# Narrow TensorE tiles for the small products of a delta-rule decoder layer

## The chip, the cores and the metric

The kernel runs on one core of a Trainium2 chip. The metric is the time of one execution on the device, in microseconds (us). The median of three runs before the change is 1135.75 us (1135.46 to 1139.98). TensorE (PE in the rows; PEld is its weight load) multiplies, VectorE (DVE), ScalarE (ACT) and GpSimd (POOL) work on elements, SyncE (SP) issues most loads.

## What is computed

One layer of a decoder for a prompt of 512 tokens with 16 learned meta tokens in front, and for 8 samples of 8 new tokens each. The layer has differential attention and a gated delta rule side by side on one normalised input, gates that merge them, and a gated feed-forward net with a short convolution. The change lies in the delta rule. It has 4 heads, and per head a matrix state of 128 by 128 for the prompt and one for each of the 8 samples. Cut to what matters:

```python
def l2norm(x):
    return xf * lax.rsqrt(jnp.sum(xf * xf, axis=-1, keepdims=True) + 1e-6)

qkv, new_gdn_conv = causal_dwconv(gdn_qkv, gdn_conv_buf, p['gdn_conv_w'])   # its last 3 rows are an output
qkv = jax.nn.silu(qkv)
gq = l2norm(gq) * (GDN_DK ** -0.5)
gk = l2norm(gk)
beta = jax.nn.sigmoid(gdn_b)
g = -jnp.exp(a_log) * jax.nn.softplus(gdn_a + dt_bias)
...
gcum = jnp.cumsum(gc, axis=-1)
decay = jnp.exp(jnp.where(causal, gcum[..., :, None] - gcum[..., None, :], -jnp.inf))
...
v_new = u_i - jnp.einsum('bhcd,bhde->bhce', w_i, s)
o = einsum('bhcd,bhde->bhce', q_i * exp(g_i), s) + einsum('bhce,bhef->bhcf', intra, v_new)
s = s * exp(g_last) + einsum('bhcd,bhce->bhde', k_i * exp(g_last - g_i), v_new)
```

All data is fp32. What the outputs need of it here: the states after the step, the last rows before the convolution, and the layer's result.

## The kernel before

Tokens lie in columns in most stages: columns 0 to 511 are the prompt, then 64 of the samples (8 by 8), then 16 meta tokens. The prompt is cut into four chunks of 128 tokens; samples and meta tokens form a fifth chunk of 80 (`NTL`).

Large products are made with split operands: an fp32 number is written as `hi + lo` of the type fp32r, and a product is three passes (`project`, L350: hi by hi, hi by lo, lo by hi). Small products use plain fp32 operands. Every product goes through `mm` (L270), which also adds an estimate of its length to `self.work`.

The order: `embed` normalises and transposes the tokens; `da_queries` makes the queries; `gdn_scalars` (L514) projects beta and decay (8 columns of the input projection, weights `bahi` and `balo`, result `bat`, which is transposed chunk by chunk) and computes the log decay `g`; `gdn_decays` (L591) sums it. Then two streams run against each other: `main`, which does the prompt's attention (`da_main`) with the first head's delta-rule projection, and then the four delta-rule heads (`gdn`, L688); and `rest`, which does the samples' attention over cached pages, the gates and one output branch. `merge` (L280) takes the next step from the stream that is furthest behind its share; once the heads have begun, `main` goes first whenever it isn't in a delay. A step `yield DELAY[i]` says that the stream isn't to go on until so much estimated TensorE work of other streams has been put in between. Below that, the compiler's scheduler orders each engine's instructions by what is ready, so a product can slip between two others of the program.

Within a head, `gdn_project` (L699) makes keys, queries and values of the next head in three parts; each part ends in `conv_tile` (L638), which does the convolution and copies the last 3 rows of the prompt and of each sample into the tile `tail`. Its inner function `rest` transposes that tile, copies it out and stores it with two DMAs on GpSimd's queue.

`gdn_chain` (L734) is the chain of a head. The steps that matter here, in order:

- L745 to L769: `gu` is the masked decay of the four chunks (128 by 512); a product with a matrix of ones (L766) spreads the running decay over rows; VectorE subtracts the column's own.
- L780 to L817: keys, queries and values are transposed; ScalarE sums the squares into `ss`. `rsqrt` (L382) is one VectorE step and one power on GpSimd; it is called for the keys and for the queries, 5 columns each (L809). From the roots come `kc` and `cq`; `kc` scales the keys.
- `gdn_base` and `gdn_solve` invert the triangular system.
- L845 to L861: the keys and queries of the 8 samples times the 8 states. `zk` holds for each sample a block of 128 columns that is zero but for 8 key and 8 query columns, so eight products (L851) over the whole array add up in one bank.
- L879 to L896: `vm` holds the new values of all samples in a mask of 8 blocks; two products over 512 columns (L895) make the updates of four states each, and VectorE adds them (L896). `states()` is called in the chain's second step (L909); the product after it is L912.

Products write to PSUM banks by tag (L153): "g" has two, "t" three, "d" two.

```python
BANKS = {"d": 2, "t": 3, "g": 2, "s": 1, "m": 1}
```

## Time and profile before

| what | value |
|---|---|
| median of three runs | 1135.75 us |
| the profiled execution | 1136.37 us |
| its span, first to last instruction | 1134.6 us |
| mean granted TensorE clock in the span | 0.998 |
| TensorE busy | 1112.5 us (98%) |
| VectorE busy | 729.3 us (64%) |
| ScalarE busy | 524.7 us (46%) |
| GpSimd busy | 225.8 us (20%) |
| four delta-rule heads | about 228 to 592 us of the span |

How to read the rows. In a timeline, a row has the start in us from the span's start, the length from the start of its first to the end of its last instruction, engine, line, operation, `out<-in` by the program's names, rows by columns of the weights and of the moving operand, and the count of instructions that were merged into it; in square brackets, the engine's idle time before it and what ended that. All products carry the helper's line L273 and all transposes L421, so one goes by tile names. Lengths of matmuls overlap: the time that a group takes from TensorE is read from its start to the start of the next group. In rows of one tile, three numbers in ns are the shortest, the median and the longest; then the starts of the first and the last, and the shapes. A table of windows has the length of the stretch, then each engine's busy time with the count of its instructions, the granted clock, and the DMA's share and GB/s.

### The profile page before, as it was taken

The page shows a single profiled execution, that of the slowest core. Times are in us where ns is not written, and L with a number is a line of the kernel's source. Part 1 is how long each engine was busy: PE and PEld are TensorE (multiplying, and loading weights), DVE is VectorE, ACT ScalarE, POOL GpSimd, SP SyncE. Part 2 cuts the span into 40 slices and gives each one's busy share as a digit, 9 for nine tenths or more (in the row PEclk, how much of TensorE's full clock was granted, in tenths as well). Part 3 has the DMA queues.
Part 4 walks back from the last instruction along what each step waited for, and adds up shares of the span by engine and source line. Part 5 has one row for each costly group of instructions (what it writes and reads, how often), then busy time and mean ns, then how long its engine had stood idle before and what let it go on. Part 6 is the DMA issues. An engine that isn't in the chain of part 4 may idle for free.

```text
span 1134.6 us, 22730 instructions
## 1 busy us (share of the span) xinstructions
PE 1112.5 (98%) x8263; PEld 976.8 (86%) x8263; DVE 729.3 (64%) x1891; ACT 524.7 (46%) x1264; POOL 225.8 (20%) x344
## 2 busy tenths in 40 slices
PE   8999999999999999999999999999999999999997
PEld 6987887787787787689999987899999999988886
DVE  5456666696486377375335575599999999752315
ACT  5244544464365365352324244464555555842311
POOL 3122221020120020010000003344444454300000
PEclk9999999999999999999999999999999999999999
DMA  6376336837846866733234344333333332333213
GB/s 193 83 235 199 102 92 200 261 103 251 246 147 224 283 178 223 251 87 87 50 90 118 105 146 135 102 102 95 94 95 95 95 100 84 116 108 108 84 48 120
DMA packets 167610, 156.97 MB, mean 138 GB/s; under 512 B 12540, under 2 KB 123715, under 8 KB 167498
## 3 DMA queue, kind: packets, MB, share of 16 engines
q1 hardware_dynamic: 162833, 147.14, 42.5%
q0 software_dynamic: 3264, 5.16, 1.5%
q10 hardware_dynamic: 1400, 3.22, 0.9%
q8 instruction: 65, 1.06, 0.4%
q14 instruction: 48, 0.39, 0.1%
HBM read 145.60 MB, written 9.88 MB: 137 GB/s over the span
## 4 chain that ended last, share of the span: by engine, by line
PE 82%; DVE 7%; issue 3%; ACT 3%; POOL 3%; DMA 2%; SPq 0%; DVEq 0%; POOLq 0%; ACTq 0%
PE ps_d L273 32%; PE ps_t L273 20%; PE ps_g L273 16%; PE ps_s L273 7%; PE ps_t L421 6%; ACT KT L1421 1%; PE ps_m L273 1%; DVE wlo L316 1%; DVE cy L672 1%; POOL grr L385 1%; DMA wraw<-in_w_ffn_in 1%; DMA page<-in_cache_v 0%; DVE gf L1745 0%; DVE fy L1926 0%; DVE row L992 0%
## 5 line engine op out<-in xcount | busy, mean ns | idle before, releaser
L273 PE MATMUL ps_d<-xhi,whi 128*128 128x256 f32 (+2 forms) x704 | 217.3, 309 | 0.6 <-ACT xhi L315 0.5
L273 PE MATMUL ps_d<-xhi,wlo 128*128 128x256 f32 (+2 forms) x704 | 213.0, 303 | 0.5 <-POOL wlo L316 0.5
L273 PE MATMUL ps_d<-xlo,whi 128*128 128x256 f32 (+2 forms) x704 | 212.4, 302 | 0.3 <-DVE xlo L316 0.3
L316 DVE TENSOR_TENSOR wlo<-wraw,whi 128x512 fp32r<-128x512 f32 x190 | 143.5, 772 | 107.2 <-ACT whi L315 106.3
L315 ACT CAST whi<-wraw 128x512 fp32r<-128x512 f32 x194 | 116.5, 621 | 163.7 <-PE ps_d L273 69.4
L273 PEld LDWEIGHTS ps_d<-xhi,whi 128*128 128x128 f32 x704 | 133.1, 189 | 6.2 <-issue 3.8
L273 PEld LDWEIGHTS ps_d<-xlo,whi 128*128 128x128 f32 x704 | 133.4, 190 | 3.2 <-issue 2.4
L273 PEld LDWEIGHTS ps_d<-xhi,wlo 128*128 128x128 f32 x704 | 133.2, 189 | 2.4 <-issue 1.0
L316 DVE TENSOR_TENSOR lw<-sw,hw 128x512 fp32r<-128x512 f32 x76 | 69.8, 918 | 5.2 <-ACT hw L315 5.2
L1421 ACT COPY KT<-ps_t 128x512 f32<-128x512 f32 x106 | 57.2, 603 | 31.6 <-PE ps_t L421 31.1
L421 PE MATMUL ps_t<-consts,page 128*128 128x128 f32 x512 | 67.8, 279 | 0.5
L273 PE MATMUL ps_t<-fhit,hw 128*128 128x290 f32 x228 | 68.1, 299 | 0.1
L273 PE MATMUL ps_t<-flot,hw 128*128 128x290 f32 x228 | 67.7, 297 | 0.0
L273 PE MATMUL ps_t<-fhit,lw 128*128 128x290 f32 x228 | 67.7, 297 | 0.0
L421 PEld LDWEIGHTS ps_t<-consts,page 128*128 128x128 f32 x512 | 55.5, 140 | 14.1 <-issue 7.0
L315 ACT CAST hw<-sw 128x512 fp32r<-128x512 f32 x76 | 46.7, 617 | 18.5 <-PE ps_g L273 12.2
L273 PEld LDWEIGHTS ps_t<-fhit,hw 128*128 128x128 f32 x228 | 43.0, 189 | 0.4 <-DVE p L1949 0.4
L273 PEld LDWEIGHTS ps_t<-flot,hw 128*128 128x128 f32 x228 | 43.3, 190 | 0.0
L273 PEld LDWEIGHTS ps_t<-fhit,lw 128*128 128x128 f32 x228 | 43.1, 189 | 0.0
L1924 ACT ACTIVATE fy<-fpre,fw 128x592 f32<-128x592 f32 x22 | 19.5, 884 | 46.3 <-DVE fpre L1884 46.3
L1926 DVE SCALAR_TENSOR_TENSOR fy<-fpre,fw,fy 128x592 f32<-128x592 f32 x44 | 36.5, 829 | 1.0 <-ACT fy L1924 0.3
L273 PE MATMUL ps_s<-page,pT 128*32 128x256 f32 x512 | 35.1, 385 | 2.0 <-DMA page<-in_cache_v 1.8
(691 smaller groups left out, 2870.0 us busy)
## 6 DMA issues: line engine op xcount, KB each, us to landing
page<-in_cache_k SPq DMA_DIRECT2D x128, 256.0 KB, 4.4
page<-in_cache_v SPq DMA_DIRECT2D x128, 256.0 KB, 4.2
wraw<-in_w_in SPq DMA_DIRECT2D x88, 256.0 KB, 3.1
wraw<-in_w_ffn_in SPq DMA_DIRECT2D x50, 256.0 KB, 3.0
wraw<-in_w_down SPq DMA_DIRECT2D x44, 256.0 KB, 2.8
raw<-in_w_ffn_in SPq DMA_DIRECT2D x38, 256.0 KB, 2.9
wraw<-in_w_out SPq DMA_DIRECT2D x16, 256.0 KB, 3.2
x<-in_x_prompt SPq DMA_DIRECT2D x4, 512.0 KB, 6.8
```

The costliest lines, as they stand in the source:

```text
L273: return self.nc.tensor.matmul(out, lhsT, rhs, **kw).ins
L315: self.nc.scalar.copy(hi, raw)
L316: (eng or self.nc.vector).tensor_tensor(out=lo, in0=raw, in1=hi.bitcast(F32), op=ALU.subtract)
L385: nc.gpsimd.tensor_tensor(out=dst, in0=dst, in1=self.mhalf[:rows, :n], op=ALU.pow)
L421: self.nc.tensor.transpose(out, in_, self.ident[:k, :k])
L672: nc.vector.scalar_tensor_tensor(out=y, in0=pre[:, j : j + n], scalar=self.cw[:, ch, 24 + j : 25 + j], in1=y, op0=ALU.mult, op1=ALU.add)
L1421: copy(kt[:, :, 128 * j : 128 * j + 128], tp)
L1924: nc.scalar.activation(y, pre[:, 0:592], AF.Identity, bias=fw[:, m, 19:20], scale=fw[:, m, 16:17])
L1926: nc.vector.scalar_tensor_tensor(out=y, in0=pre[:, j : j + 592], scalar=fw[:, m, 16 + j : 17 + j], in1=y, op0=ALU.mult, op1=ALU.add)
```

## The change

- Beta and decay: the weights are no longer split. They lie in a tile of 32 columns per block of the contraction, 8 of them filled and the rest zero; each product uses 32 columns of the array, four of them side by side (`32 * (k % 4)`), plain fp32, once for the hi and once for the lo part of the tokens: 32 products for 48. The four partial sums come out in four groups of 32 partitions; the transpose of a chunk becomes a product with a 0/1 matrix `sums`, which also adds them.
- The matrix of ones is a tile of its own of type fp32r, filled on GpSimd, and no longer part of the constants.
- Row decays: `g` is split into `ghi` and `glo`; two masked tiles are made of them on VectorE and two fp32r products are added for one fp32 product.
- Conv tails: the three parts of a head share one tile `tail` of 81 columns; after the third part one transpose, one copy and four stores follow, for three, three and six.
- Roots: one `rsqrt` over 10 columns for two over 5.
- Keys and queries times states: sixteen products with 32 columns of weights, in four column tiles (keys of samples 0 to 3 and 4 to 7, queries likewise), for eight over the whole array.
- Updates of the samples' states: the masked values have 4 blocks for 8, made by one VectorE instruction for two; the two products take rows 0 to 31 and 32 to 63, in two row tiles and two banks, both issued before the first addition.
- In the prompt's attention, the small transpose L1346 takes 128 columns for 16.

The delays, the shares of the streams and the banks are as before.

```diff
@@ gdn_scalars
-        hi = self.t(pool, [128, 8, 8], "bahi", F32R)
-        lo = self.t(pool, [128, 8, 8], "balo", F32R)
-        nc.vector.tensor_copy(hi, raw)
-        nc.vector.tensor_tensor(out=lo, in0=raw, in1=hi.bitcast(F32), op=ALU.subtract)
-        bat = self.t(pool, [8, NT], "bat")
+        wide = self.t(pool, [128, 8, 32], "baz")
+        nc.gpsimd.memset(wide, 0.0)
+        nc.gpsimd.tensor_copy(wide[:, :, 0:8], raw)
+        bat = self.t(pool, [128, NT], "bat")
         for c in HALF_T:
-            p = self.ps("d")[:8, : c[1] - c[0]]
-            self.project(p, ([hi[:, k] for k in range(8)], [lo[:, k] for k in range(8)]), self.x, c)
+            p = self.ps("d")[:, : c[1] - c[0]]
+            for j, x in enumerate(self.part(self.x, c)):
+                for k in range(8):
+                    r = slice(32 * (k % 4), 32 * (k % 4) + 32)
+                    self.mm(p[r], wide[:, k], x.bitcast(F32)[:, k], start=j == 0 and k < 4, stop=j == 1 and k >= 4)
             self.evac_tokens(bat, p, c, nc.vector.tensor_copy)
...
-            self.transpose(p[:n, i, :], bat[:, c0 : c0 + n])
+            self.mm(p[:n, i, :], bat[:, c0 : c0 + n], self.c("sums"), start=True, stop=True)
...
+        one = self.t(pool, [128, 128], "one")
+        nc.gpsimd.memset(one, 1.0)
+        nc.gpsimd.tensor_copy(self.ones, one)
+        self.ghi, self.glo = (self.t(self.keep, [128, 4, H], f"g{p}", F32R) for p in ("hi", "lo"))
+        nc.vector.tensor_copy(self.ghi, self.g[:, 0:4])
+        nc.vector.tensor_tensor(out=self.glo, in0=self.g[:, 0:4], in1=self.ghi.bitcast(F32), op=ALU.subtract)
@@ conv_tile and gdn_project
-        def rest():
-            tp = self.ps("t")
-            self.transpose(tp[:27, :128], tail)
-            rows = self.t(pool, [27, 128], "tailT", bufs=2)
...
+    def conv_tails(self, h, tail):
+        nc, pool = self.nc, self.gproj
+        tp = self.ps("t")
+        self.transpose(tp[:81, :128], tail)
+        rows = self.t(pool, [81, 128], "tailT")
+        nc.vector.tensor_copy(rows, tp[:81, :128])
+        sl = slice(128 * h, 128 * h + 128)
+        to = self.o["new_gdn_conv_prompt"][0, 0].rearrange("j (p c) -> p j c", p=3)[:, :, sl]
+        nc.gpsimd.dma_start(to, rows[0:9])
+        for p in range(3):
+            to = self.o["new_gdn_conv_sample"][0, :, :, 512 * p + 128 * h : 512 * p + 128 * h + 128]
+            nc.gpsimd.dma_start(to.rearrange("b j c -> (b j) c"), rows[9 + 24 * p : 33 + 24 * p])
...
         yield DELAY[0]
-        rest()
+        self.conv_tails(h, tail)
@@ gdn_chain
-        gu = self.t(pool, C4, "dd")
-        nc.vector.tensor_tensor(
-            out=gu, in0=self.c("upper").unsqueeze(1).to_broadcast(C4), in1=cols(self.g), op=ALU.mult
-        )
+        gus = []
+        for g, tag, bufs in ((self.ghi, "dd", 1), (self.glo, "lm", 2)):
+            gu = self.t(pool, C4, tag, F32R, bufs=bufs)
+            nc.vector.tensor_tensor(
+                out=gu, in0=self.c("upper").unsqueeze(1).to_broadcast(C4), in1=cols(g.bitcast(F32)), op=ALU.mult
+            )
+            gus.append(gu)
...
-        self.mm(rp, self.c("ones"), gu, start=True, stop=True)
+        for j, gu in enumerate(gus):
+            self.mm(rp, self.ones, gu, start=j == 0, stop=j == 1)
...
-        for e in range(2):
-            self.rsqrt(rr[:, e], ss[:, e], 0.25, EPS, 128, 5)
+        self.rsqrt(rr.rearrange("p e c -> p (e c)"), ss.rearrange("p e c -> p (e c)"), 0.25, EPS, 128, 10)
...
-        for b in range(NB):
-            self.mm(
-                p[:, :128], self.zk[:, 128 * b : 128 * b + 128], state[:, b], start=b == 0, stop=b == NB - 1
-            )
+        for j in range(4):
+            for e in range(4):
+                b = j + 4 * (e % 2)
+                self.mm(
+                    p[32 * e : 32 * e + 32, :128], self.zk[:, 128 * b + 32 * e : 128 * b + 32 * e + 32], state[:, b],
+                    start=j == 0, stop=j == 3,
+                )
...
-            for b4, vm in vms:
-                hp = self.ps4("g")
-                self.mm(hp, kp[:64, 4], vm[:64].rearrange("p b v -> p (b v)"), start=True, stop=True)
+            hps = [self.ps4("g") for _ in range(2)]
+            for e, hp in enumerate(hps):
+                r = slice(32 * e, 32 * e + 32)
+                self.mm(hp, kp[r, 4], vm[r].rearrange("p b v -> p (b v)"), start=True, stop=True)
+            for e, hp in enumerate(hps):
+                b4 = slice(4 * e, 4 * e + 4)
                 nc.vector.tensor_tensor(out=state[:, b4], in0=state[:, b4], in1=hp, op=ALU.add)
@@ prompt_rows
-            self.transpose(tq[:NM, :128], at[:, 0:NM])
+            self.transpose(tq[:, :128], at[:, 0:128])
```

More of the change, by code (lines that the diff above doesn't have):

```diff
@@ L66, in _lay_out_constants @@
     put("ident", np.eye(128))
-    put("ones", np.ones((128, 128)))
     put("upper", i[:, None] <= i[None, :])
@@ L199, in run @@
         self.ident = self.consts[:, 0:128]
+        self.ones = self.t(self.cpool, [128, 128], "ones", F32R)
         self.mhalf = self.t(self.cpool, [128, 32], "mhalf")
@@ L599, in gdn_decays @@
         p = self.ps("t")[:, : 8 * nch].rearrange("p (c e) -> p c e", e=8)
-        for e, (whole, tail) in enumerate((("upper", "upper_t"), ("ones", "same_t"))):
+        for e, (whole, tail) in enumerate(((self.c("upper"), "upper_t"), (self.ones.bitcast(F32), "same_t"))):
             sl = slice(4 * e, 4 * e + 4)
-            self.mm(p[:, 0:4, sl], self.c(whole), self.g[:, 0:4, :], start=True, stop=True)
+            self.mm(p[:, 0:4, sl], whole, self.g[:, 0:4, :], start=True, stop=True)
             self.mm(p[:NTL, 4, sl], self.c(tail, NTL), self.g[:NTL, 4, :], start=True, stop=True)
@@ L636, in gdn_consts, with conv_tile @@
         nc.vector.tensor_scalar(self.gnorm, self.gnorm, 0.5, None, op0=ALU.mult)
-    def conv_tile(self, ps, ch, dp, dt):
+    def conv_tile(self, ps, ch, dp, dt, tail):
         nc, pool = self.nc, self.gproj
@@ L707, in gdn_project @@
         outs = {0: (full(q), q[:, CS:NT]), 1: (full(kt), kt[:, CS:NT]), 2: (full(vt), vt[:, CS:NT])}
-        rest = None
+        tail = self.t(pool, [128, 81], "tail")
         for part in (1, 0, 2):
@@ L712, in gdn_project @@
             yield from self.dense_steps(wt, self.x, HALF_T[0], out)
-            if rest:
-                rest()
             yield 0.0
             yield from self.dense_steps(wt, self.x, HALF_T[1], out)
-            rest = self.conv_tile(out, 4 * part + h, *outs[part])
+            self.conv_tile(out, 4 * part + h, *outs[part], tail)
             yield 0.0
         yield DELAY[0]
-        rest()
+        self.conv_tails(h, tail)
     def gdn_gate(self, h, z2):
@@ L753, in gdn_chain @@
         rt = self.ps("g")
-        self.mm(rt[:, :NTL], self.c("ones", NTL), gut, start=True, stop=True)
+        self.mm(rt[:, :NTL], self.ones.bitcast(F32)[:NTL], gut, start=True, stop=True)
         nc.scalar.activation(er[:, CS:NT], rt[:, :NTL], AF.Exp)
```

32 lines of the change are left out of this document (12 added, 20 removed).

## The prediction

> **What bounds the kernel now.** I read the page first, then the busy time by stage, then single stretches of the timeline of TensorE and of VectorE.
>
> ```profile
> span 1134.6 us, 22730 instructions
> PE 1112.5 (98%) x8263; PEld 976.8 (86%) x8263; DVE 729.3 (64%) x1891; ACT 524.7 (46%) x1264; POOL 225.8 (20%) x344
> ...
> PE 82%; DVE 7%; issue 3%; ACT 3%; POOL 3%; DMA 2%; SPq 0%; DVEq 0%; POOLq 0%; ACTq 0%
> ```
>
> ```profile
> core 0: us, PE busy (x) PEld busy (x) DVE busy (x) ACT busy (x) POOL busy (x), PEclk, DMA share, GB/s
> 42.60:49.10 6.50, 6.50 (x50) 4.14 (x47) 2.52 (x9) 1.41 (x3) 0.00 (x0) 1.00 0.34 82
> 228.00:592.00 364.00, 357.39 (x3091) 300.39 (x3092) 220.08 (x729) 172.46 (x478) 39.69 (x63) 1.00 0.55 171
> 592.00:644.00 52.00, 51.40 (x384) 51.08 (x383) 26.76 (x49) 18.82 (x38) 0.00 (x0) 1.00 0.41 117
> ```
>
> TensorE is busy 98% of the span and 82% of the chain of waits; the chain names no other engine with more than 7%. The three windows are the stage of beta and decay, the four delta-rule heads, and what follows them. In the four heads TensorE lacks only 364.0 - 357.4 = 6.6 us although VectorE works 220 us there: while one head's chain waits, projections, pages and gates fill in. The filler isn't used up when the chain ends, for the next 52 us are again full (51.4). So a microsecond of TensorE saved in these stages should come off the end, as long as the chain doesn't become the longer of the two. "Busy" counts overlapping matmuls with their latency, so I price each group by its start and the start of what follows it.
>
> **The prices.** A plain fp32 product is two records in these rows, a product of split (fp32r) operands one.
>
> Beta and decay take 48 split products now, from the first row to the second, 49.13 - 42.62 = 6.51 us:
>
> ```profile
> 42.62 0.28 PE L273 MATMUL ps_d<-xhi,bahi 128*8 128x256 f32 x1
> ...
> 49.13 0.29 PE L421 MATMUL ps_t<-consts,bat 8*128 8x8 f32 x2
> ```
>
> Afterwards they are 32 fp32 products in four column tiles of 32. The kernel has such products already:
>
> ```profile
> 441.22 1.07 PE L273 MATMUL ps_s<-KT,qb 128*32 128x256 f32 x16
> 442.22 1.31 PE L421 MATMUL ps_t<-consts,page 128*128 128x128 f32 x10
> ...
> 180.27 1.93 PE L273 MATMUL ps_s<-page,pT 128*32 128x256 f32 x32
> 182.13 0.65 PE L421 MATMUL ps_t<-consts,S 128*128 128x128 f32 x4
> ```
>
> Eight take 1.00 us and sixteen 1.86, so a round of four over 256 columns costs 0.43 and a stretch 0.14 once. The change has four rounds over 256 columns and four over 336 (0.43 x 336/256 = 0.56): 1.72 + 2.26 + 0.14 = 4.1 us, 2.4 saved. The five transposes of the result (0.11 each, as the conv tails below) become fp32 products with 128 weight columns. The nearest is the folding product, four in 0.89 us:
>
> ```profile
> 355.77 1.05 PE L273 MATMUL ps_t<-consts,xy 128*128 128x32 f32 x8
> 356.66 0.37 PE L273 MATMUL ps_d<-xlo,whi 128*128 128x256 f32 x1
> ```
>
> Five times 0.22 instead of 0.11 gives back 0.6: **1.8 us saved**, 1.0 to 2.4 at the ends. The new weights tile is filled on GpSimd, whose queue stood empty for 31.0 us before this row, so it is ready in time. Without that cover its two steps, each about as long as that row, cost 0.7 us once.
>
> ```profile
> 50.79 0.34 POOL L643 COPY pre<-cw 128x24 f32<-128x24 f32 x2 [31.01 <-DVE cw L633]
> ```
>
> Keys and queries times the states, eight products a head:
>
> ```profile
> 369.71 2.05 PE L273 MATMUL ps_g<-st,zk 128*128 128x128 f32 x16
> 371.60 0.71 PE L421 MATMUL ps_t<-consts,S 128*128 128x128 f32 x5
> ...
> 554.60 1.95 PE L273 MATMUL ps_g<-st,zk 128*128 128x128 f32 x16
> 556.30 0.37 PE L273 MATMUL ps_d<-xhi,whi 128*128 128x256 f32 x1
> ```
>
> That is 1.89 and 1.70 us. Sixteen narrow ones in four rounds over 128 columns cost 4 x 0.215 + 0.14 = 1.0. I take 0.9 a head, **3.6 us saved**; 0.7 a head, 2.8, is the low end.
>
> The update of the samples' states is two products over 512 columns:
>
> ```profile
> 294.62 1.98 PE L273 MATMUL ps_g<-lm,kn 64*128 64x512 f32 x4
> 296.53 0.49 PE L273 MATMUL ps_g<-grhs,xy 128*128 128x128 f32 x2
> ...
> 295.78 0.69 DVE L896 TENSOR_TENSOR st<-st,ps_g 128x512 f32<-128x512 f32 x1 [1.50 <-PE ps_g L273]
> 296.64 0.69 DVE L896 TENSOR_TENSOR st<-st,ps_g 128x512 f32<-128x512 f32 x1 [0.17 <-PE ps_g L273]
> ...
> 573.53 0.39 PE L273 MATMUL ps_d<-xhi,whi 128*128 128x256 f32 x1
> 573.87 0.38 PE L273 MATMUL ps_g<-grhs,xy 128*128 128x128 f32 x2
> ```
>
> 1.91 us. Afterwards they lie in two row tiles of 32 rows and two banks. The row tiles that the trace has are the two score maps:
>
> ```profile
> 74.56 0.94 PE L273 MATMUL ps_m<-kT,qT 64*128 64x400 f32 x4
> 75.43 1.07 PE L273 MATMUL ps_s<-KT,qb 128*32 128x256 f32 x16
> ...
> 76.94 0.49 PE L273 MATMUL ps_m<-kT,qT 64*128 64x128 f32 x4
> 77.36 0.42 PE L273 MATMUL ps_d<-xhi,wlo 128*128 128x336 f32 x1
> ```
>
> A pair over 400 columns takes 0.87, over 128 columns 0.42, so over 512 about 0.87 + 112 x 0.45/272 = 1.06: 0.85 a head saved on TensorE. But "g" has two banks, and the chain's next product (L912) needs the first again once VectorE has added it. That add began 1.16 us after the matmul and took 0.69, and the second matmul covered it: L912 started at 296.53, as the add ended. Now nothing of its own covers it, and unless filler slips in TensorE waits 0.8 us and nothing is gained. Behind L912 stand the chain's next copy and the new state; their turn is unchanged, as the add ends when it did. The last two rows are the fourth head, where a projection's products did slip in between the updates and L912; in the first they did not. So I take half, **1.7 us saved**, 0 to 3.4 at the ends.
>
> The row decays are one fp32 product over 512 columns and become two split ones:
>
> ```profile
> 312.12 1.06 PE L273 MATMUL ps_g<-dd,consts 128*128 128x512 f32 x2
> 313.02 0.60 PE L421 MATMUL ps_t<-consts,kt 128*128 128x128 f32 x4
> ...
> 668.43 0.62 PE L273 MATMUL ps_t<-owhi,gt 128*66 128x512 f32 x2
> 668.89 0.39 PE L273 MATMUL ps_t<-owlo,gt 128*66 128x512 f32 x1
> ```
>
> 0.90 against 0.46 for two: 0.44 a head, **1.8 us saved**. For it VectorE makes a second product a head (0.69, first row below) ahead of the chain's first matmuls:
>
> ```profile
> L746 DVE TENSOR_TENSOR dd<-consts,g x4: 672/688/694, 228.8 to 463.0; 128x512 f32<-128x512 f32 x4
> L883 DVE TENSOR_TENSOR lm<-gv,consts x8: 672/679/684, 288.9 to 560.6; 64x512 f32<-64x512 f32 x8
> L385 POOL TENSOR_TENSOR grr<-grr,mhalf x8: 1162/1203/1797, 239.4 to 501.7; 128x5 f32<-128x5 f32 x8
> L554 POOL TENSOR_TENSOR sqb<-beta,half x1: 3543/3543/3543, 52.3 to 52.3; 128x20 f32<-128x20 f32 x1
> ```
>
> It gets one masked copy of the same length back later (L883, eight to four). Filler covers the later start; bare, it would cost 4 x 0.69 = 2.8. The two splits of the decay are small VectorE work beside projections, and the ones on GpSimd are filled long before a head: nothing.
>
> The conv tails are twelve transposes in the trace and become four; one takes 0.11:
>
> ```profile
> 233.10 0.27 PE L421 MATMUL ps_t<-consts,tail 128*27 128x128 f32 x1
> 233.21 0.27 PE L421 MATMUL ps_t<-consts,kt 128*80 128x128 f32 x1
> ```
>
> **0.9 us saved**. Their stores on GpSimd's queue go from 24 to 16 and now stand together behind one copy; only the next head's masks and powers are behind them, long after. The wider transpose in the prompt's attention writes 128 rows for 16 with the same stream of 128 columns: nothing.
>
> One root for keys and queries: a power over 5 columns takes 1.20, over 20 columns 3.54, so over 10 about 2.0. Where the scaled keys waited for both powers (2.4) they come 0.4 earlier, where for the first alone 0.8 later. A delay filled with projections follows, so I take nothing; bare, between 1.7 gained and 3.1 lost over four heads.
>
> [...] Each new narrow stretch (two, four and four) has paid only the 0.14 read above in my sum. [...] The rows with 1.00 and 1.86 have entry and exit in them and speak for the small price.
>
> **The sum.** 1.8 + 3.6 + 1.7 + 1.8 + 0.9 = 9.8 us. The profiled execution took 1136.4 us (span 1134.6 and 1.8 around it), so 1126.6; it lies 0.6 above the median of the runs, 1135.75, so the forecast for the median is **1126 us**. All low ends together (1.0, 2.8, 0, 1.8 - 2.8, 0.9 - 3.1) give 0.6 saved, all high ends (2.4, 3.6, 3.4, 1.8, 0.9 + 1.7) 13.8, that is 1135 and 1122.
>
> **The rivals.** First, the heads' chain takes the gain back: the state products and the updates run sooner but the copies, adds and powers behind them don't, and TensorE waits there. Only 1.8 + 1.8 + 0.9 = 4.5 is kept: 1131.2, a little under no change. For it speaks the add that ends just as L912 starts; against it that only 6.6 us were idle in 364.
>
> Second, and on the other side: the tiles run one after another, so the change doesn't do what it says. At 0.43 for each narrow product of 256 columns, beta and decay would take 16 x 0.43 + 16 x 0.56 = 15.8 instead of 6.5, the states 16 x 0.215 = 3.4 instead of 1.8 a head, the updates gain nothing: 9.3 + 6.4 + 0.6 - 1.8 - 0.9 = 13.6 lost, 1149. It is slower from the point where fewer than about 1.8 tiles overlap. Against it: eight narrow products in 1.00 us are 3.4 at once, though these tiles hold other weights and rows of 32, not 64.
>
> [...]
>
> **How the numbers follow.** Forecast 0.70 (own range 1122 to 1130), chain 0.18, drain 0.05, one after another 0.07. A measurement of this kernel can tell about 0.5% from no change, 5.7 us here: faster is below 1130.1, slower above 1141.4. Faster: 0.70 + 0.05 of the chain case + 0.03 of the drain = 0.78; slower 0.07; the same 0.15. The range runs from 1121, just under all high ends, to 1135, all low ends; it leaves out the serial case and some of the chain's.
>
> **What would show it.** Right: beta and decay near 4.1 us from first to last product, the states near 1.0 and the updates near 1.1 a head, the rest of the timeline unchanged but earlier. The updates' term is wrong if the wait before L912 exceeds 0.5 us in all heads. The root's is wrong if TensorE waits before the transposes of the scaled keys. The whole is wrong if idle time in the four heads rises well over 6.6 us, or if a narrow round costs 1.7 us and not 0.43.

## The result and the profile after

The change made the kernel slower. The median went from 1136.98 us (11 runs, 1135.46 to 1139.98) to 1143.73 us (11 runs, 1139.80 to 1150.32), a ratio of 1.0068 with a 95% interval of 1.0050 to 1.0085. The forecast was 1126, the range 1121 to 1135. The profiled execution of after took 1148.56 us, with a span of 1146.8, 12.2 more than before.

The page of after, its span, its busy times and the head of its chain of waits:

```profile
span 1146.8 us, 22863 instructions
PE 1116.5 (97%) x8340; PEld 980.7 (86%) x8340; DVE 728.5 (64%) x1879; ACT 524.8 (46%) x1264; POOL 219.7 (19%) x336
...
PE 83%; DVE 6%; ACT 5%; DMA 2%; issue 2%; POOL 1%; DVEq 0%; SPq 0%; ACTq 0%; POOLq 0%
```

The shares hardly differ from before. But TensorE's busy time rose by 4.0 us although its work was to fall, and its idle time, span less busy time, by 8.2 (22.1 to 30.3). The timeline of TensorE in after shows what the parts cost:

```profile
43.93 1.07 PE L274 MATMUL ps_d<-xhi,baz 128*32 128x256 f32 x16
...
46.20 1.34 PE L274 MATMUL ps_d<-xhi,baz 128*32 128x336 f32 x16 [0.34 <-DVE qm L1164]
...
48.60 0.61 PE L274 MATMUL ps_t<-consts,bat 128*128 128x8 f32 x4
...
314.61 0.50 PE L274 MATMUL ps_g<-dd,ones 128*128 128x512 f32 x1
...
315.17 0.28 PE L274 MATMUL ps_d<-xhi,whi 128*128 128x256 f32 x1
...
576.36 1.08 PE L274 MATMUL ps_g<-st,zk 128*32 128x128 f32 x32
577.38 0.41 PE L274 MATMUL ps_d<-xhi,whi 128*128 128x322 f32 x1
...
594.56 1.13 PE L274 MATMUL ps_g<-lm,kn 32*128 32x512 f32 x4
595.62 0.39 PE L274 MATMUL ps_d<-xhi,whi 128*128 128x256 f32 x1
```

From start to the start of what follows: beta and decay 48.60 - 43.93 = 4.7 us with a wait of 0.34 in it (4.1 was forecast) up to the folding products, a head's row decays 0.56 (0.46), keys and queries times states 1.02 (1.0; serial tiles would take 3.4 by the prediction's estimate), the updates 1.06 (1.06). So the tiles do run side by side, and the stretches are about as short as forecast. The time went elsewhere. Two views show where. The first is what TensorE waited for, from 228 to 596 us, in before (three of its eight lines, the longest and the last among them) and in after (six of its ten longest):

```profile
engine line waited for: us in total, times, longest us
PE ps_t L421 <- DVE on L935: 2.0, 2, 1.3
PE ps_t L421 <- DVE kn L814: 1.2, 1, 1.2
...
PE ps_g L273 <- DVE dtbig_up L964: 0.2, 1, 0.2
```

```profile
PE ps_d L274 <- DVE wlo L317: 1.9, 1, 1.9
PE ps_t L422 <- DVE kn L826: 1.7, 2, 1.4
PE ps_t L422 <- DVE kn L827: 1.1, 1, 1.1
PE ps_g L274 <- DVE grhs L918: 0.9, 2, 0.4
PE ps_g L274 <- ACT gv L881: 0.8, 1, 0.8
...
PE ps_g L274 <- DVE st L910: 0.8, 1, 0.8
```

The eight lines of before add up to 5.3 us, the ten longest of after alone to 9.7. The waits for the scaled keys (`kn`) grew from 1.2 us to 2.8. New are the waits for a projection's split weights (`wlo`), for steps of the third head's chain (`grhs`, `gv`), and for the bank before L912 (`st`), which the prediction had named. The second view is the windows of after in which the granted clock (third number from the right) was low:

```profile
51.34:54.76 3.42, 3.42 (x18) 3.42 (x18) 0.75 (x5) 1.94 (x4) 2.66 (x1) 0.50 0.02 5
416.57:419.98 3.41, 3.36 (x15) 3.37 (x16) 2.87 (x7) 1.73 (x10) 0.00 (x0) 0.50 0.63 163
481.42:495.08 13.66, 12.86 (x57) 8.97 (x52) 5.93 (x18) 4.13 (x14) 1.54 (x2) 0.50 0.35 97
```

In 20.5 us TensorE ran at a granted clock of 0.50, which is by estimate (half of 20.5) up to 10 us of lost work; in before the only such window begins at 1130.97 and lasts to the end. That explains the busy time: the first update product of the third head takes 1.12 us just ahead of such a window (480.22) and the second 2.07 in it (483.05). The spread of the change's runs goes with it too, from 1140.1 us at a mean clock of 0.998 to 1150.3 at 0.988. But the runs at 0.997 and 0.998 are still 3 to 5 us above before, so the clock isn't all of it.

### The profile page after: what moved, and what is told of

It is laid out like the page before. It is cut to its first block, busy times and chain, and to the rows that moved or that the text cites. A ratio compares the mean times of both kernels' runs of the same rounds, so it can differ in the third digit from the quotient of the medians.

```text
span 1146.8 us, 22863 instructions
## 1 busy us (share of the span) xinstructions
PE 1116.5 (97%) x8340; PEld 980.7 (86%) x8340; DVE 728.5 (64%) x1879; ACT 524.8 (46%) x1264; POOL 219.7 (19%) x336
## 4 chain that ended last, share of the span: by engine, by line
PE 83%; DVE 6%; ACT 5%; DMA 2%; issue 2%; POOL 1%; DVEq 0%; SPq 0%; ACTq 0%; POOLq 0%
PE ps_d L274 32%; PE ps_t L274 20%; PE ps_g L274 15%; PE ps_s L274 7%; PE ps_t L422 7%; ACT KT L1435 2%; PE ps_m L274 1%; DVE wlo L317 1%; DMA page<-in_cache_v 1%; DMA wraw<-in_w_branch_a 1%; ACT whi L316 1%; POOL grr L386 0%; DVE lw L317 0%; DVE gf L1759 0%; DVE fy L1940 0%
## 5 line engine op out<-in xcount | busy, mean ns | idle before, releaser
L274 PE MATMUL ps_d<-xhi,whi 128*128 128x256 f32 (+2 forms) x704 | 220.1, 313 | 0.4 <-ACT xhi L316 0.3
L274 PE MATMUL ps_d<-xhi,wlo 128*128 128x256 f32 (+2 forms) x704 | 215.5, 307 | 1.9 <-DVE wlo L317 1.9
L274 PE MATMUL ps_d<-xlo,whi 128*128 128x256 f32 (+2 forms) x704 | 215.3, 306 | 0.1
L274 PEld LDWEIGHTS ps_d<-xhi,whi 128*128 128x128 f32 x704 | 136.1, 193 | 6.4 <-issue 3.3
L274 PEld LDWEIGHTS ps_d<-xlo,whi 128*128 128x128 f32 x704 | 136.5, 194 | 3.2 <-issue 2.4
L274 PEld LDWEIGHTS ps_d<-xhi,wlo 128*128 128x128 f32 x704 | 135.7, 193 | 3.4 <-DVE wlo L317 2.2
L274 PE MATMUL ps_s<-KT,qb 128*32 128x256 f32 x512 | 36.7, 385 | 0.8
```

The costliest lines, as they stand in the source:

```text
L274: return self.nc.tensor.matmul(out, lhsT, rhs, **kw).ins
```

## The experiments

Theory F, formed from these two views: the merged conv tails lower the planner's account of TensorE work, so the order of the steps changes, the third head's output gate moves behind the head's chain, and TensorE runs bare. Theory N: the narrow tiles themselves cost time or clock. All kernels were timed beside runs of the kernel before (medians 1136.65 to 1137.11).

| label | median us | ratio to before, 95% interval |
|---|---|---|
| acct_alone | 1144.48 | 1.0070 (1.0056 to 1.0084) |
| acct_kept | 1142.52 | 1.0049 (1.0036 to 1.0063) |
| tails_alone | 1144.41 | 1.0078 (1.0056 to 1.0100) |
| all_but_tails | 1144.02 | 1.0062 (1.0043 to 1.0081) |
| tails_account_kept | 1139.45 | 1.0017 (1.0007 to 1.0026) |
| root_alone | 1140.84 | 1.0037 (1.0022 to 1.0052) |
| states_alone | 1140.26 | 1.0026 (1.0013 to 1.0040) |
| updates_alone | 1134.73 | 0.9979 (0.9966 to 0.9992) |
| beta_alone | 1136.71 | 0.9998 (0.9985 to 1.0011) |
| decays_alone | 1149.37 | 1.0101 (1.0085 to 1.0116) |
| updates_and_beta | 1136.99 | 0.9999 (0.9988 to 1.0009) |
| updates_beta_tails | 1140.39 | 1.0025 (1.0014 to 1.0035) |
| decays_queries_later | 1144.00 | 1.0064 (1.0050 to 1.0078) |
| all_queries_later_account | 1140.28 | 1.0026 (1.0013 to 1.0038) |
| all_but_tails_queries_later | 1139.67 | 1.0023 (1.0012 to 1.0034) |
| all_queries_later | 1139.92 | 1.0021 (1.0011 to 1.0031) |
| masked_product_twice | 1140.03 | 1.0036 (1.0022 to 1.0050) |
| decays_lo_on_gpsimd | 1142.93 | 1.0044 (1.0031 to 1.0058) |

**The account.** First the planner's account alone, with every instruction kept:

```diff
             self.transpose(tp[:27, :128], tail)
+            if ch // 4 != 2:
+                self.work -= 0.11
```

> Not one instruction differs from the kernel before; only the planner's account of TensorE work is 0.11 us lower for two of the three transposes of a head's conv tails (0.88 us over four heads), as the change lowers it. Theory F (the account moves the third head's gate to behind that head's chain, the chain runs bare and TensorE idles): the chip takes about as much longer here as the change falls short of the forecast, 1143.7 - 1126 = 17 us, so 1148 to 1155, with the products of the fourth head's output gate ahead of the third head's in the trace and over 10 us of idle or slowed TensorE between keys and queries times states and the last step of the third head. Rival N (the narrow tiles cost more than forecast or bring the granted clock down): as before, 1137, clock 0.998.

It took 1144.48 us, 0.7% more than before: 8 us lost to an estimate. The loss is half of what F expected. The output transposes of the first three heads start 3.5, 5.3 and 9.0 us later than before (310.9 to 314.4, 402.4 to 407.7, 488.7 to 497.7), but part of that is other streams' work done earlier: from each head's output transposes to the next head's TensorE idles 1.3 us in the first head (counted from its first row-decay product), 3.8, 6.0 and 0.1, where before it was 1.6, 2.4, 1.9 and 0.2. So the third head loses most, 4.0 us of idle time, though not the 10 that F named. Its gate moved as F says. ScalarE's copies of the gates' products, in before (`z` is the third head's gate) and here (`gt` is a gate of `rest`):

```profile
450.99 0.40 ACT L730 ACTIVATE z<-ps_d 128x256 f32<-128x256 f32 x1
470.96 0.45 ACT L730 ACTIVATE z<-ps_d 128x322 f32<-128x322 f32 x1
```

```profile
491.67 0.37 ACT L1520 ACTIVATE gt<-ps_d 128x256 f32<-128x256 f32 x1
494.32 0.38 ACT L732 ACTIVATE z<-ps_d 128x256 f32<-128x256 f32 x1 [2.29 <-PE ps_d L273]
498.26 0.43 ACT L732 ACTIVATE z<-ps_d 128x322 f32<-128x322 f32 x1
```

The gate's products, done at 451 and 471 before, are done at 494 and 498, behind a piece of the next gate. What stood inside the chain now stands behind it, and the window after 470 us, before and then here, shows the hole:

```profile
470.00:480.00 10.00, 10.00 (x78) 6.51 (x76) 3.86 (x10) 2.33 (x11) 0.94 (x1) 1.00 0.90 268
```

```profile
470.00:480.00 10.00, 8.38 (x74) 5.67 (x74) 4.29 (x10) 4.16 (x15) 0.00 (x0) 1.00 0.79 234
```

TensorE (the first busy column) lacks nothing there before and 1.6 us here. Then the other way round, the whole change with the account given back:

```diff
+            if part != 1:
+                self.work += 0.11
             yield 0.0
             yield from self.dense_steps(wt, self.x, HALF_T[1], out)
```

> The change as it is, with 0.22 us a head given back to the planner's account for the two transposes that fell away. Theory F: the third head's gate lies inside its chain again, and the forecast's saving shows: 1125 to 1130, clock 0.998. Rival N: still about 1140 to 1144 with a clock of 0.99, since every narrow stretch is there.

1142.52 us: 12 or more above the 1125 to 1130 that F expected, though the third head's gate is back inside the chain. So the tails' account isn't the whole cause. But it is the smaller part of what the change takes off the account. `mm` (L270) counts 1.68 ns a column for an fp32 product with more than 32 columns of weights and 0.42 for any other:

```python
self.work += (1.68e-3 if lhsT.dtype == F32 and lhsT.shape[1] > 32 else 0.42e-3) * n
```

By this rule the change also lowers the account by 0.86 us a head for the keys and queries times states (8 x 128 columns at 1.68 become 16 x 128 at 0.42) and by 0.43 for the row decays (512 at 1.68 become twice 512 at 0.42), against 0.22 for the tails. No run gives these two back, so how much of the loss is the account as a whole stays untested. The merged tails without any narrow tile (the change's `conv_tails` in the kernel before):

```diff
-            rest = self.conv_tile(out, 4 * part + h, *outs[part])
+            self.conv_tile(out, 4 * part + h, *outs[part], tail)
...
+        self.conv_tails(h, tail)
```

> The kernel before with the merged conv tails alone; no narrow tile anywhere. Theory F: slower by 10 us or more, 1147 to 1155, as the account falls. Rival N: 1136, 0.9 less than before.

1144.41 us, 3 below F's range, and just what the account alone costs. The change with the old tails (that hunk undone):

```diff
+            if rest:
+                rest()
...
-        self.conv_tails(h, tail)
+        rest()
```

> The change without the merged conv tails: all narrow tiles, the split row decays and the one root stay. Theory F: 1126 to 1131, 0.9 above the change with the account kept. Rival N: 1141 to 1145.

1144.02 us: no better than the change, and 13 above F's range. With acct_kept this says that the other parts lose as much without the tails as with them. And the merged tails with the account kept (the `tails_alone` edit and the one of `acct_kept`):

```diff
+            if part != 1:
+                self.work += 0.11
...
+        self.conv_tails(h, tail)
```

> The kernel before with the merged conv tails, and 0.22 us a head given back to the planner's account. The prediction's term: 0.9 saved, 1135.9. Theory F says the same, since the gate stays in the third head's chain: 1135 to 1137, about 8 us below the merged tails without the account. Rival (the merged tails themselves cost time: their later stores or the later transpose): 1142 or more.

1139.45 us, 2 above before and 5 below the same without the account: the account is most of the tails' loss, and a loss of 0.07 to 0.26% is left where 0.9 us were to be gained.

**Each part alone.** The one root:

```diff
-        for e in range(2):
-            self.rsqrt(rr[:, e], ss[:, e], 0.25, EPS, 128, 5)
+        self.rsqrt(rr.rearrange("p e c -> p (e c)"), ss.rearrange("p e c -> p (e c)"), 0.25, EPS, 128, 10)
```

> The kernel before with the one root over 10 columns alone; TensorE's program order is the one of before but for a few products. The prediction's term: 0, so 1136.7. Theory K (the keys wait for the whole power, 2.0 us in place of 1.2, and other VectorE steps get ahead of their scaling, so TensorE waits before the transposes of the scaled keys): 1 to 3 us slower, 1138 to 1140, with 0.8 us and more of added wait before those transposes in two or more heads.

1140.84 us, 0.22 to 0.52% slower, and 0.8 above K's range. The power over 10 columns and the waits for the keys' scaling, in root_alone:

```profile
L385 POOL TENSOR_TENSOR grr<-grr,mhalf x4: 1984/2712/3192, 240.4 to 504.3; 128x10 f32<-128x10 f32 x4
```

```profile
PE ps_t L421 <- DVE kn L813: 2.3, 3, 1.0
...
PE ps_t L421 <- DVE kn L814: 1.2, 1, 1.2
```

The power takes 2.0 to 3.2 us, median 2.7, where the prediction had 2.0 and before 1.2; the waits for `kn` went from 1.2 us to 3.5. TensorE's order is the one of before here but for three score products, so most of this loss is the wait for the power, as K says, and not a new order of TensorE: from the first row-decay product to the fourth head's output transposes TensorE idles 9.4 us, before 6.2. Keys and queries times states:

```diff
+        for j in range(4):
+            for e in range(4):
+                b = j + 4 * (e % 2)
+                self.mm(p[32 * e : 32 * e + 32, :128], self.zk[:, 128 * b + 32 * e : 128 * b + 32 * e + 32], state[:, b], start=j == 0, stop=j == 3)
```

> The kernel before with the column-tiled keys and queries times states alone; the order shifts in places since both the account and the products are shorter. The prediction's term: 3.6 saved, 1133.1, with about 1.0 us a head from first to last of these products. Theory F (a shorter stretch of TensorE work inside the chain leaves the chain as long, and the reshuffled order loses cover): nothing saved or up to 4 us slower, 1136.7 to 1141, though the stretch itself is 1.0 us.

1140.26 us, slower by 0.13 to 0.40%, with the stretch at 1.0 us as forecast. All waits of 0.2 us and more from 228 to 596 add up to 9.3 us, against 5.3; 2.4 of them are for transposed pages (`KT`) that ScalarE copies out, of which before has none in its list. The updates:

```diff
+            hps = [self.ps4("g") for _ in range(2)]
+            for e, hp in enumerate(hps):
+                r = slice(32 * e, 32 * e + 32)
+                self.mm(hp, kp[r, 4], vm[r].rearrange("p b v -> p (b v)"), start=True, stop=True)
```

> The kernel before with the two row-tiled state updates alone; TensorE's program order is unchanged but for three products. The prediction's term: 1.7 saved, 1135.0 (0 to 3.4: 1133.3 to 1136.7). Rival (the wait for the bank takes more than the narrow products save): 1137 to 1139.

1134.73 us, 0.08 to 0.34% faster, near the term of 1.7 us. The wait for the bank that the prediction halved the term for is there, 0.78, 0.27, 0.59 and 0.40 us in the four heads. The first head's updates and L912 behind them:

```profile
294.77 1.13 PE L273 MATMUL ps_g<-lm,kn 32*128 32x512 f32 x4
296.68 0.49 PE L273 MATMUL ps_g<-grhs,xy 128*128 128x128 f32 x2 [0.78 <-DVE st L895]
```

From the first update to L912 it takes 1.91 us, as before, and so it does in the second and third heads; only the fourth, where gate products follow, has 1.06 for 1.91. So the profiled execution shows next to nothing of the gain where it should be: from the first row-decay product to the fourth head's output transposes it takes 366.0 us, before 366.2. Beta and decay:

```diff
+                    self.mm(p[r], wide[:, k], x.bitcast(F32)[:, k], start=j == 0 and k < 4, stop=j == 1 and k >= 4)
...
+            self.mm(p[:n, i, :], bat[:, c0 : c0 + n], self.c("sums"), start=True, stop=True)
```

> The kernel before with the column-tiled beta and decay alone; TensorE's program order is unchanged. The prediction's term: 1.8 saved, 1134.9. Rival (the stage starts later for its weights, and the split projections after it wait): 1136.7, nothing saved.

The first page transpose comes 1.7 us earlier (62.0 to 60.3, and the stage starts at 42.6 in both) and the fourth head's output transposes 1.3 (595.95 to 594.61): the stage saves about what was forecast. In the median, 1136.71 us, it doesn't show (0.9985 to 1.0011). In the change itself the same stretch is 19.0 us, only 0.4 less than before, since a window at half clock lies in it (51.34 to 54.76). The row decays:

```diff
+        for g, tag, bufs in ((self.ghi, "dd", 1), (self.glo, "lm", 2)):
...
+        for j, gu in enumerate(gus):
+            self.mm(rp, self.ones, gu, start=j == 0, stop=j == 1)
```

> The kernel before with the row decays of split operands alone. The prediction's term: 1.8 saved, 1135.0. Rival (the second masked product delays the head's first VectorE steps and the order shifts, so the waits of TensorE in the four heads grow by more than 1.8 us): 1137 to 1141.

1149.37 us: 12 us lost by a part that was to save 1.8, more than the whole change loses. In TensorE's timeline of the first head, before and then here:

```profile
244.93 0.32 PE L273 MATMUL ps_d<-xhi,wlo 128*128 128x336 f32 x1
245.08 0.67 PE L421 MATMUL ps_t<-consts,kn 80*128 80x80 f32 x5
```

```profile
240.48 0.32 PE L273 MATMUL ps_d<-xlo,whi 128*128 128x336 f32 x1
245.43 0.37 PE L421 MATMUL ps_t<-consts,kn 80*128 80x80 f32 x1 [4.64 <-DVE kn L824]
...
247.69 0.56 PE L273 MATMUL ps_d<-xhi,wlo 128*128 128x256 f32 x1
```

Before, projection products fill TensorE to the very start of the keys' transposes. Here 44 of them stand behind the transposes, and TensorE waits 4.64 us. VectorE's timeline, before and then here, says what for:

```profile
237.65 0.67 DVE L316 TENSOR_TENSOR wlo<-wraw,whi 128x512 fp32r<-128x512 f32 x1
...
238.33 0.68 DVE L316 TENSOR_TENSOR wlo<-wraw,whi 128x512 fp32r<-128x512 f32 x1
```

```profile
243.02 0.17 DVE L821 TENSOR_TENSOR kc<-grr,hsb 128x5 f32<-128x5 f32 x1 [1.09 <-POOL grr L385]
244.16 0.17 DVE L823 TENSOR_SCALAR cq<-grr 128x5 f32<-128x5 f32 x1 [0.97 <-POOL grr L385]
244.24 0.85 DVE L678 SCALAR_TENSOR_TENSOR cy<-pre,cw,cy 128x616 f32<-128x616 f32 x1
245.01 0.28 DVE L824 TENSOR_SCALAR kn<-kn,kc 80x128 f32<-80x128 f32 x1
...
246.58 0.68 DVE L316 TENSOR_TENSOR wlo<-wraw,whi 128x512 fp32r<-128x512 f32 x1
```

The keys' factor `kc` is there at 243.2, but the scaling of the keys stands behind the queries' factor, which waits 0.97 us for its own power on GpSimd, and behind a step of the convolution. The 44 products could not have filled the wait: the first of them needs the split weights `wlo`, which VectorE makes at 246.58, behind the scaled keys; in the kernel before it makes them at 237.65 and 238.33. So what moved is VectorE's order, and the cover went with it. From 243.59 to 250.42 us the clock was 0.50, and TensorE was busy 4.67 us of that, so by estimate (half of 4.67) up to 2.3 us more were lost.

**Parts together.** The updates with beta and decay (both diffs above), and these with the merged tails and the account kept:

```diff
+                r = slice(32 * e, 32 * e + 32)
+                self.mm(hp, kp[r, 4], vm[r].rearrange("p b v -> p (b v)"), start=True, stop=True)
...
+                    self.mm(p[r], wide[:, k], x.bitcast(F32)[:, k], start=j == 0 and k < 4, stop=j == 1 and k >= 4)
```

> The kernel before with the state updates in row tiles and beta and decay in column tiles, nothing else. These two left the order as it was. If single parts add up as measured (2.1 and 0.1 saved): 1134.5; by the prediction's terms (1.7 and 1.8): 1133.2. Rival: the gain of either is lost in noise and the kernel is as before, 1136.8.

> Updates in row tiles, beta and decay in column tiles, and the merged tails with the account kept. By the prediction's terms 1.7 + 1.8 + 0.9 saved: 1132.4. By the single parts as measured, with the tails at 0.9: 1133.7. Rival (each further reshuffle of the order costs more than the tails save): 1136 or more.

1136.99 and 1140.39 us. The updates' gain alone isn't there when beta and decay go with it, so both gains are unproven, and the tails take 3 us again. In updates_and_beta TensorE's order is still that of before but for these parts' own products. Of the six parts, these two and the root are the ones that leave a head's account as it was; the tails, the states and the row decays lower it, and in their runs other products moved in many places. That points to the account and doesn't prove it. Single parts don't add up either: alone they lose or gain 8.9, 4.2, 3.0, -2.4, -0.2 and 11.5 us (ratio less one, times 1137), 25 together, and the change loses 8.

**The order.** Theory O: these losses are the order that the compiler makes, not the parts' work. The queries' root is moved behind the keys' step, so that nothing of it can stand ahead of the keys' scaling in program order:

```diff
-        for e in range(2):
-            self.rsqrt(rr[:, e], ss[:, e], 0.25, EPS, 128, 5)
+        self.rsqrt(rr[:, 0], ss[:, 0], 0.25, EPS, 128, 5)
...
         nc.vector.tensor_tensor(out=kp[:, 0:4], in0=kn[:, 0:4], in1=cols(self.ek), op=ALU.mult)
+        self.rsqrt(rr[:, 1], ss[:, 1], 0.25, EPS, 128, 5)
+        cq = self.t(pool, [128, 5], "cq")
```

> The split row decays alone, with the queries' root and its scale moved behind the keys' (after the step that follows the transposes of the scaled keys). Theory O (the 12 us of the split decays alone are an order: 44 projection products stand behind the transposes of the scaled keys, which wait 5 us for VectorE's queue, and the clock halves): TensorE's order has the products ahead of the transposes again, the wait of 4.6 us is gone, 1135 to 1139. Rival (the second masked product and the split itself cost it): still 1146 or more.

1144.00 us. The long wait is gone and the products stand ahead of the transposes again, with 5 of the 12 us; 7 are left, so O holds for part of it. In the trace the first head (first row-decay product to output transposes) is still 3.0 us longer than before and the third (from the second's output transposes) 2.7, of which 3.0 and 2.0 are idle time of TensorE. The largest wait of TensorE now, from 228 to 610 us:

```profile
PE ps_d L273 <- DVE wlo L316: 2.6, 3, 0.9
```

The projection products in front of the transposes wait for their own split weights, which VectorE makes. The same edit in the whole change, with the account kept, without the tails, and as the change is:

> The whole change but with two roots, the queries' root moved behind the keys' step, and the account of the tails kept. Theory O: the order has its cover in the first and the third head, so most of the forecast's sum shows: 1128 to 1133. Rival N (the parts themselves cost more than forecast): 1139 or more.

> The change without the merged tails, with two roots and the queries' root moved behind the keys' step. Theory O: 1130 to 1135, against 1144 of the change without the tails; in the third head the order has the old cover, in VectorE's order the queries' scale stands ahead of the keys' once, in the third head. Rival N: 1140 to 1145.

> The whole change, with two roots and the queries' root moved behind the keys' step, the account as in the change. Theory F for the third head (its gate still stands behind its chain): the first head's order is mended, the third's isn't, 1136 to 1142, that is 6 to 10 us above the same with the account kept. Rival (the account no longer matters once the keys go first): within 2 us of the same with the account kept.

1140.28, 1139.67 and 1139.92 us. All three are 3 us slower than before and 4 faster than the change. The first is 7 above what O expected, the second 5; the third lies in F's range, but not 6 to 10 above the first. So the tails' account makes no difference in this order, against F. The profiled run of the third was its slowest, 1146.57 us, with one window at a clock of 0.50 of 20.5 us (472.28 to 492.76) in the third head; the medians agree all the same. The first head isn't mended by this edit: in all_queries_later_account TensorE idles 5.8 us in it, before 1.6, the largest part again for `wlo` (1.9 us in two waits); over the four heads it is 13.7 against 6.2.

**VectorE's load.** The windows of before show a load that the prediction had averaged away:

```profile
228.00:268.00 40.00, 39.27 (x353) 33.41 (x354) 37.53 (x141) 24.56 (x68) 8.54 (x17) 1.00 0.50 161
268.00:308.00 40.00, 39.40 (x371) 28.98 (x371) 15.92 (x49) 17.33 (x51) 2.48 (x5) 1.00 0.73 223
```

In the first head's first 40 us VectorE (the third busy column) works 37.5 us, in the next 40 only 15.9; the first 40 us of the other heads hold 35.7, 37.1 and 31.3. Theory V: work added there comes on top. The kernel before with the masked product made twice:

```diff
+        for _ in range(2):
             nc.vector.tensor_tensor(
                 out=gu, in0=self.c("upper").unsqueeze(1).to_broadcast(C4), in1=cols(self.g), op=ALU.mult
             )
```

> The kernel before, but VectorE makes the masked decay of each head twice into the same tile: 0.69 us more VectorE work at the start of each head, TensorE's work unchanged and its order unchanged from the second head on. The prediction's step (filler covers the later start): 1136.8. Theory V (VectorE is as full as TensorE in the first 40 us of a head, so its work there comes on top): 0.69 or more in each of four heads, 1139.5 to 1143. The starts of later milestones show it head by head.

1140.03 us, the time that V expected, but not head by head. The first row-decay product and the output transposes of the first, third and fourth heads, before and then here:

```profile
229.76 0.35 PE L273 MATMUL ps_g<-gut,consts 80*128 80x80 f32 x2
310.90 0.70 PE L421 MATMUL ps_t<-consts,on 128*128 128x128 f32 x5 [0.74 <-DVE on L935]
...
488.71 0.73 PE L421 MATMUL ps_t<-consts,on 128*128 128x128 f32 x5 [1.27 <-DVE on L935]
595.95 0.67 PE L421 MATMUL ps_t<-consts,on 128*128 128x128 f32 x5
```

```profile
228.19 0.35 PE L273 MATMUL ps_g<-gut,consts 80*128 80x80 f32 x2
314.02 0.70 PE L421 MATMUL ps_t<-consts,on 128*128 128x128 f32 x5 [0.73 <-DVE on L936]
492.46 0.73 PE L421 MATMUL ps_t<-consts,on 128*128 128x128 f32 x5 [1.27 <-DVE on L936]
599.72 0.67 PE L421 MATMUL ps_t<-consts,on 128*128 128x128 f32 x5
```

The first head starts 1.6 us earlier than before and ends 3.1 later: 4.7 us lost for 0.69 us of work. The second loses 0.6, the third and the fourth nothing (3.75 and 3.77 behind). From the second head on TensorE's order is the one of before; in the first it differs, and a window of 3.41 us at a clock of 0.50 lies in it (246.94 to 250.35). So V, which asked for 0.69 or more in each, falls for the last two heads: where the order stayed, the cover swallowed the work there. This is the clearest run for the order, though what order and load each cost in the first head isn't told apart: TensorE's idle time in it grew by 1.9 us, 1.4 of them one wait for the scaled keys, and the half clock costs by estimate up to 1.7 (half of the 3.41). Last, the split decays with the second masked product on GpSimd:

```diff
-        for g, tag, bufs in ((self.ghi, "dd", 1), (self.glo, "lm", 2)):
+        for eng, g, tag, bufs in ((nc.vector, self.ghi, "dd", 1), (nc.gpsimd, self.glo, "lm", 2)):
```

> As the split decays with the queries' root later (1144.0), but the second masked product on GpSimd. Theory V: the load on VectorE is gone, so 3 to 7 us less, 1137 to 1141. Rival (the order alone, or GpSimd's slower product in front of the row decays): 1143 or more.

1142.93 us, 1 to 2 below the same with both on VectorE and 2 above V's range, and the intervals overlap (1.0031 to 1.0058, 1.0050 to 1.0078). It tells little: the waits for `wlo` fell from 2.6 to 0.8 us, and others took their place.

## Why the prediction was wrong

- **Beta and decay, 1.8:** held in the trace of beta_alone (1.7 at the first page), not provable in the median. **States, 3.6:** the stretch is 1.02 us as worked out; its gain didn't reach the end. **Updates, 1.7:** the stretch is 1.06 us where other work follows, but in updates_alone the wait before L912 took the gain whole in three heads of four, so half was too much for the heads. **Row decays, 1.8:** 0.56 for 0.46, so 0.34 a head as a stretch. The rival of serial tiles is out: the states' stretch is 1.02 us, not 3.4. A drain of TensorE at each stretch, to which the chances give 0.05, is a term that no run shows: each stretch has its entry and exit in it, and the states and the updates take 1.02 and 1.06 where 1.0 and 1.06 were forecast, beta and decay, with the wait of 0.34 taken off, 4.3 for 4.1.
- **Conv tails, 0.9:** wrong in sign. "Only the next head's masks and powers are behind them" looked at GpSimd's queue; what is behind a transpose is also the estimate that it adds to the planner's account. With no instruction changed, that estimate costs 0.56 to 0.84%.
- **One root, 0:** a term mis-sized. The prediction took 2.0 us for the power and a delay filled with projections as its cover. The power took 2.7 in the median, the waits for the keys grew by 2.3 us, and alone the root costs 0.22 to 0.52%, 2.5 to 5.9 us; the worst end was 3.1. TensorE waits before the transposes of the scaled keys, which the prediction had named as the sign against this term.
- **The step that failed** is the one under the sum, "the rest of the timeline unchanged but earlier", and beside it "filler covers the later start". Both take the order of the work as given. It isn't: the order comes from estimates and from what the compiler finds ready. The tails, the states and the row decays lower the estimates, by 1.51 us a head together, which the sum put at nothing without a reason, and they moved products across the chain's waits, the row decays VectorE's steps too. Idle time of TensorE in the four heads rose from 6.6 us to 14.8 (386.0 us from 228 to 614, 371.2 busy), which the prediction had named as the sign that it is wrong and which is all of the 8.2 us by which its idle time grew; the other 4.0 us of the longer span are busy time, with 20.5 us at half clock in it.
- **The rival of the chain** had the right place, but its price, all gains of the chain lost and no more, was too small: 4.5 us were to be kept and 7 were lost. Lost cover cost more than the work that was saved, and the clock added to it.
- **What stays open:** shown are the account (8 us without any instruction changed), the first head with a new order, load and clock together (4.7 us for 0.69 us of work, 0 to 0.6 in the heads where the order stayed), the root's wait, and 5 of the split decays' 12 us. Not shown is how much of the change's loss is the account of the states and the row decays, which no run kept; why the whole change with the queries' root moved is still 3 us slower than before, some 14 above the forecast; and what made the idle time that is left of the split decays. No order was found that keeps both the parts and the cover. The wider transpose of the prompt's attention, put at nothing, wasn't run alone; in before the transposes of `S` with 16 columns of weights took 274 ns in the mean, those with 128 columns 279. Of all kernels run only updates_alone lay below before by more than the noise, by 0.08 to 0.34%, and its gain isn't located in its trace.

## What to carry to other kernels

Where steps are placed by estimates or by a scheduler, a cheaper instruction is an edit of the whole order: compare the order of the long products around every wait before and after, and price the cover that moved, not only the instruction that shrank. A busy share averaged over heads hides stages in which a second engine is nearly as full as the first (here 37.5 and 39.3 of 40 us); read it in windows as long as the chain's phases. Time the cheaper instruction once with its old estimate kept, so that its work and its order are told apart; here that was done for the smallest of three. And put a change's parts alone on the chip early: here a part that saves TensorE work cost more than the whole change.

## What was not expected of the hardware

The granted clock fell to 0.50 in single windows. Those in the traces named here, but for the one at the end of before (from 1130.97) and of after (from 1143.6), were about 3.41 us long or a small multiple (3.42, 3.41 and 13.66 in after, 3.41 in masked_product_twice, 6.83 in decays_alone, 20.48 in all_queries_later), and in decays_alone it began at 243.59, in the middle of the long wait of 4.64 us. No idle stretch of that length went before: in the 3.41 us ahead of the window TensorE was busy 0.62 us in decays_alone, 1.56 and 2.61 in the heads of after, and before the one at 51.34 all the time. And the half clock stayed while TensorE was busy: 481.42 to 495.08 has it busy 12.86 of 13.66 us, with the chain's short products first and gate products in the last 3 us. What brings the half clock about, no run here shows. The author's guess is that a bare stretch of a chain can bring it about and is then paid for twice, in some runs only (those of after have mean clocks from 0.988 to 0.998); it is read from where the windows lie and wasn't tested.
